# Hybrid decoder block: turned tiles leave PSUM first, a second turn stands elsewhere, one weight form is added on VectorE, and the last norm is regrouped

## The chip, the cores and the metric

The kernel runs on one core of one Trainium2 chip. The metric is the device time of one execution in microseconds (us), the median of several runs. TensorE (PE in the profile) multiplies, VectorE (DVE) and ScalarE (ACT) do the elementwise work, GpSimd (POOL) issues some DMAs here, and SyncE (SP) issues the rest. Each engine takes its own instructions strictly in order and waits on semaphores for the others.

## What is computed

One decoder block over 512 tokens of width 1024 in float32, and a final RMSNorm. The reference, cut to its frame and to the part in which the change lies:

```python
def swiglu(u, w_gate_up, w_down):          # FF = 2816
    gate, up = jnp.split(u @ w_gate_up, 2, axis=-1)
    return (jax.nn.silu(gate) * up) @ w_down

def reference(x, mem, ...):
    h = x
    for l in range(DEPTH):                 # DEPTH = 1
        h = h + hybrid_mixer(rmsnorm(h, mix_norm[l]), ...)
        h = h + memory_cross_attention(rmsnorm(h, xattn_norm[l]), rmsnorm(mem, mem_norm[l]), ...)
        h = h + swiglu(rmsnorm(h, ffn_norm[l]), w_gate_up[l], w_down[l])
    return rmsnorm(h, final_norm)
```

## The kernel before

The mixer and the attention fill the first 425 us or so, the feed-forward part and the last norm the rest. The mixer and the attention are not touched. Every product of two float32 matrices is taken in three matmuls: each operand is split in a high part and the rest, and high by high, high by rest and rest by high are summed in PSUM. For the weights `split_unit` does this with a ScalarE cast (`whi`, L194) and a VectorE subtraction (`wlo`, L196).

**The feed-forward part saves an eighth of its matmuls.** Each product of 2x2 blocks is computed by seven block products in place of eight. The seven need weight *forms* that are sums of quarters of the weight, and *forms* of the activations, which `forms` makes (L1116 on). Gate and up are computed in five blocks g0 to g4 of 512 columns each and a narrow block g5 of 256. The down product is taken in three parts, d0 after g1, d1 after g3, d2 after g5. The matmuls of both carry line L1046, and write PSUM tiles called gA, gB, gC and dA, dB, dC.

**Weight forms.** For one chunk of the weights, `load_strassen` loads the forms 1, 2 and 4 as they are (quarters 11, 12, 22), by DMAs that SP issues. Forms 5 and 7 are a load by SP and a second DMA that POOL issues and that adds to what lies there (L171). Form 6 is form 1 plus form 5, where form 1's tile is overwritten: a DMA from tile to tile that adds, issued by POOL as soon as form 2 is split (L202). Form 3 is form 2 plus form 6, a VectorE addition (L189). The whole narrow block lies in one chunk.

**Turns.** The products of silu(gate) and up lie with tokens on the partitions, and the down product wants them turned. `i_turnff` (Y in the list below) turns half a block: eight TensorE transposes (L1105, `ffT`) from the tiles `t_gu` into a PSUM tile of 128 by 1024 with the tag pd. Of this tag there is **one buffer**, so that the next turn waits until everything that reads the last has ended. ScalarE copies the second half out as `fb` (L1110); `forms` reads the first half (`FA`) straight from PSUM, in the cast L1122, in the subtractions L1131 and L1126, and last in L1141.

**Order.** The list `SPEC` says slot by slot which items are issued; each slot's matmuls stand in program order, and the elementwise work that follows an item (`post`), the loads and the splits of the next slot are written between them. Within that, a scheduler of the language places the instructions of each engine. `U:b.f` is product f of gate block b, `d:p.f` of down part p, `Y:b.i` the turn of half i of block b, `G` the load of the last gain.

**The last norm.** `i_down` adds each finished product to the residual `h` (L1202, L1204). When a half row of 128 tokens is finished, `half_done` squares it on ScalarE with a sum beside it and multiplies it by the gain (L1225). When both halves are, `final` turns the two sums to a factor (L1243, L1244, Ln, Exp, and one corrective step L1248 to L1250), scales both halves and stores them. The four token groups c = 0 to 3 are finished by product 7 (c = 2, 3) and product 4 (c = 0, 1).

Of the kernel before, what the change touches and what calls it, by code (L numbers as in the profile page):

```python
# [7 lines left out]
F32 = mybir.dt.float32  # L8
F32R = mybir.dt.float32r
AF = mybir.ActivationFunctionType  # L10
ALU = mybir.AluOpType
AX = mybir.AxisListType

P = 128
S = 512
DM = 1024
# [6 lines left out]
EPS = 1e-6  # L23
# [7 lines left out]
CHUNKS = [("g", b, ks, 512) for b in range(5) for ks in ((0, 1), (2, 3))] + [("g", 5, (0, 1, 2, 3), 256)]  # L31
# [25 lines left out]
]  # L57

# [2 lines left out]
def hybrid_block(ctx: ExitStack, tc: tile.TileContext, a: dict, out: bass.AP,  # L61
                 act_bufs=69, la=1, wb=(6, 4, 5), eng="", dact=(0, 1), raw_n=6, warm=12, spec=None, start=START, smm=START_MM, hu=1, dbg=None):
    nc = tc.nc
# [5 lines left out]
    small = ctx.enter_context(tc.tile_pool(name="small", bufs=4))  # L69
# [5 lines left out]
    def nm(base):  # L75
        uid[0] += 1
        return f"{base}_{uid[0]}"

    def T(base, dt=F32, n=512):
        return act.tile([P, n], dt, tag="a", name=nm("t_" + base))  # L80
# [101 lines left out]
    def split_unit(key):  # L182
        n = units[key][1]
        raw = ready[key]
        if key[0] == "s":
            c, f = key[1:]
            if f == 3:
                sw[c, 3] = sw.pop((c, 2))
                nc.vector.tensor_tensor(out=sw[c, 3][:, :n], in0=sw[c, 3][:, :n], in1=sw[c, 6][:, :n], op=ALU.add)  # L189
                yield  # L190
            raw = sw[c, f]
        hi = whi_p.tile([P, 1024], F32R, tag="hi", name=nm("whi"))
        lo = wlo_p.tile([P, 1024], F32R, tag="lo", name=nm("wlo"))
        nc.scalar.copy(hi[:, :n], raw[:, :n])  # L194
        yield
        nc.vector.tensor_tensor(out=lo[:, :n], in0=raw[:, :n], in1=hi.bitcast(F32)[:, :n], op=ALU.subtract)  # L196
        ready[key] = (hi, lo)
        if key[0] == "s" and f == 2:
            if (c, 5) not in sw:
                load_strassen(("s", c, 5))  # L200
            sw[c, 6] = sw.pop((c, 1))
            nc.gpsimd.dma_start(sw[c, 6][:, :n], sw[c, 5][:, :n], accum_op=ALU.add)  # L202
        yield
# [46 lines left out]
    sw = {}  # L250

    st = {}
# [842 lines left out]
    def i_turnff(b, i):  # L1095

        it = Item()

        def mm():
            it.ps = psum.tile([P, 1024], F32, tag="pd", name=nm("ffT"), bufs=1)  # L1100
            for k in (1, 0):
                for c in range(2):
                    for tt in range(2):
                        o = 512 * k + 256 * c + P * tt
                        nc.tensor.transpose(it.ps[:, o:o + P], st["fft", b, k, tt][:, (2 * i + c) * P:(2 * i + c + 1) * P],  # L1105
                                            ident)

        def post():
            fb = T("fb")
            nc.scalar.copy(fb, it.ps[:, 512:1024])  # L1110
            yield from forms("ff", 2 * b + i, it.ps[:, 0:512], fb)

        it.mm, it.post = mm, post
        return it

    def forms(x, i, FA, FB):  # L1116

        lo_, hi_ = slice(0, 256), slice(256, 512)

        def cast(base, src, w=None):  # L1120
            h = T(base, F32R)
            nc.scalar.copy(h if w is None else h[:, w], src)  # L1122
            return h

        def rest(dst, src, h):
            nc.vector.tensor_tensor(out=dst, in0=src, in1=h.bitcast(F32), op=ALU.subtract)  # L1126

        H1 = cast("xh", FA)
        H4 = cast("xq", FB[:, hi_], lo_)
        M = T("x57")  # L1130
        nc.vector.tensor_tensor(out=M[:, lo_], in0=FA[:, lo_], in1=FB[:, lo_], op=ALU.subtract)  # L1131
        nc.vector.tensor_tensor(out=M[:, hi_], in0=FB[:, hi_], in1=FB[:, lo_], op=ALU.subtract)  # L1132
        yield
        L1 = T("xl", F32R)
        rest(L1, FA, H1)
        st["X", x, 1, i], st["X", x, 2, i] = (H1[:, lo_], L1[:, lo_]), (H1[:, hi_], L1[:, hi_])
        H2 = cast("xh", M)
        N = T("x64")
        nc.vector.scalar_tensor_tensor(out=N[:, lo_], in0=M[:, lo_], scalar=-1.0, in1=FB[:, hi_],
                                       op0=ALU.mult, op1=ALU.subtract)  # L1140
        nc.vector.scalar_tensor_tensor(out=N[:, hi_], in0=N[:, lo_], scalar=-1.0, in1=FA[:, hi_],  # L1141
                                       op0=ALU.mult, op1=ALU.subtract)
        yield
        H3 = cast("xh", N)
        L2 = T("xl", F32R)
        rest(L2, M, H2)
        st["X", x, 5, i], st["X", x, 7, i] = (H2[:, lo_], L2[:, lo_]), (H2[:, hi_], L2[:, hi_])
        yield
        rest(H4[:, hi_], FB[:, hi_], H4[:, lo_])
        st["X", x, 3, i] = H4[:, lo_], H4[:, hi_]  # L1150
        L3 = T("xl", F32R)
        rest(L3, N, H3)
        st["X", x, 6, i], st["X", x, 4, i] = (H3[:, lo_], L3[:, lo_]), (H3[:, hi_], L3[:, hi_])
# [36 lines left out]
    def i_down(p, f, part=None):  # L1190
        it, ends, _ = product("d", p, f, part)

        def post():
            r, k, sign = INTO[f]
            last = p == 2
            if last and f == 2:
                st["pre"] = nc.scalar.preload_act_table_set("natural_log_exp_and_others")
                after(st["pre"], st["silu"])
            for tt in range(2):
                h = st["h", 2 * k + tt, r]  # L1200
                if sign > 0:
                    nc.vector.tensor_tensor(out=h, in0=h, in1=it.ps[tt], op=ALU.add)  # L1202
                else:
                    nc.vector.tensor_tensor(out=h, in0=h, in1=it.ps[tt], op=ALU.subtract)  # L1204
                if last and f in (2, 3):
                    half_done(2 * k + tt, r)
                elif last and f in (7, 4):
                    final(2 * k + tt)
            yield

        it.post = post if ends else None
        return it

    def number():

        st["n"] = st.get("n", -8) + 8
        if st["n"] == 0:
            st["numbers"] = T("numbers")
        return st["numbers"][:, st["n"]:st["n"] + 1]

    def half_done(c, r):
        h = st["h", c, r]
        q = number()
        nc.scalar.activation(T("sq"), h, AF.Square, accum_out=q)
        nc.vector.tensor_tensor(out=h, in0=h, in1=st["G"][r], op=ALU.mult)  # L1225
        st["ss", c, r] = q

    def i_gain():
        def prep():
# [5 lines left out]

        return Item(prep=prep)

    def final(c):
        half_done(c, 1)
        v = number()  # L1240
        y = number()
        w = number()
        nc.vector.tensor_scalar(out=v, in0=st["ss", c, 0], scalar1=1.0 / DM, scalar2=EPS, op0=ALU.mult, op1=ALU.add)  # L1243
        nc.vector.scalar_tensor_tensor(out=v, in0=st["ss", c, 1], scalar=1.0 / DM, in1=v, op0=ALU.mult, op1=ALU.add)  # L1244
        ln = nc.scalar.activation(y, v, AF.Ln)
        after(ln, st["pre"])
        nc.scalar.activation(y, y, AF.Exp, scale=-0.5)
        nc.vector.scalar_tensor_tensor(out=w, in0=v, scalar=y, in1=y, op0=ALU.mult, op1=ALU.mult)  # L1248
        nc.vector.tensor_scalar(out=w, in0=w, scalar1=-0.5, scalar2=1.5, op0=ALU.mult, op1=ALU.add)
        nc.vector.tensor_tensor(out=w, in0=w, in1=y, op=ALU.mult)  # L1250
        rows = slice(c * P, (c + 1) * P)
        for r in range(2):
            o = st["h", c, r]
            if r == 0:
                nc.scalar.activation(o, o, AF.Copy, scale=w)
            else:
                nc.vector.tensor_scalar(out=o, in0=o, scalar1=w, scalar2=None, op0=ALU.mult)
            nc.sync.dma_start(out[rows, 512 * r:512 * r + 512], o)

    def rm(r):  # L1260
        return Item(mm=r.mm, post=r.post)
# [17 lines left out]
    for line in (spec or SPEC):  # L1279
        its = []  # L1280
        for tok_ in line.split():
            name, _, arg = tok_.partition(":")
# [167 lines left out]
```

## Time and profile before

| | |
|---|---|
| median of 3 runs | 815.14 us (814.6 to 816.63) |
| the profiled execution | 817.78 us; its span, first to last instruction, 816.1 us |
| mean granted TensorE clock | 0.990 of full speed |
| busy share of the span | PE 97%, DVE 76%, ACT 59%, POOL 6% |
| chain that ended last | PE 75%, DVE 10%, DMA 7%, rest 8% |

The profile is a list of the engines' instructions in one execution, with start, length, and for idle time ahead of an instruction the length and the instruction that ended it. Starts are in us from the span's start. Matmuls overlap, so that the distance of two starts is the cost of one, and not the length shown.

### The profile page before, as it was taken

How to read it: one execution, taken by the hardware profiler on the slowest of the kernel's cores; microseconds unless marked ns; L12 is line 12 of the kernel's file. 1: busy time of each engine (PE TensorE's matmuls, PEld its weight loads, DVE VectorE, ACT ScalarE, POOL GpSimd, SP SyncE). 2: the span in 40 equal slices, each digit the busy share in tenths (PEclk: the TensorE clock that was granted, in tenths of full speed). 3: DMA queues.
4: the chain of work that ended last, by engine and by line, in shares of the span. 5: the costliest groups of instructions: out<-in, count | busy, mean ns of one | idle time of the engine just before them, and what ended most of it. 6: DMA issues, size and time to landing. Idle time of an engine off the chain costs nothing.

```text
span 816.1 us, 10514 instructions
## 1 busy us (share of the span) xinstructions
PE 791.6 (97%) x3856; PEld 666.0 (82%) x3856; DVE 617.5 (76%) x912; ACT 482.1 (59%) x768; POOL 45.6 (6%) x61
## 2 busy tenths in 40 slices
PE   9999999999999999999999999989999989999795
PEld 7888888888888889888888888878888767888684
DVE  7989979999875896355746667869657878665897
ACT  8667699567853555344635784744454835353664
POOL 0000000000000000000010001110101110101000
PEclk9999999999999999999999999999999999999899
DMA  8253415243573236223355367877887867977502
GB/s 324 86 168 104 146 55 174 65 150 100 194 250 120 81 107 192 89 78 104 129 113 145 78 207 183 235 175 190 197 256 161 256 163 178 225 221 170 138 14 103
DMA packets 40275, 124.95 MB, mean 153 GB/s; under 512 B 4752, under 2 KB 7184, under 8 KB 40224
## 3 DMA queue, kind: packets, MB, share of 16 engines
q1 hardware_dynamic: 32880, 98.33, 36.2%
q0 software_dynamic: 7344, 25.96, 17.5%
q8 instruction: 30, 0.49, 0.2%
q14 instruction: 21, 0.17, 0.1%
HBM read 113.48 MB, written 2.13 MB: 142 GB/s over the span
## 4 chain that ended last, share of the span: by engine, by line
PE 75%; DVE 10%; DMA 7%; issue 3%; ACT 3%; POOL 0%; SPq 0%; POOLq 0%; DVEq 0%; ACTq 0%
PE gA L1046 10%; PE dA L1046 5%; PE gB L1046 5%; DMA wq<-raw 4%; PE gC L1046 3%; DVE wlo L196 3%; PE v L117 2%; PE v L118 2%; PE v L116 2%; PE dB L1046 2%; DMA raw<-w_s 2%; PE op L116 2%; PE op L118 2%; PE wo L116 2%; PE wo L118 2%
## 5 line engine op out<-in xcount | busy, mean ns | idle before, releaser
L194 ACT CAST whi<-raw 128x1024 fp32r<-128x1024 f32 (+1 forms) x127 | 131.6, 1040 | 135.4 <-issue 25.6
L196 DVE TENSOR_TENSOR wlo<-raw,whi 128x1024 fp32r<-128x1024 f32 (+1 forms) x127 | 152.8, 1209 | 64.4 <-ACT whi L194 60.9
L194 ACT CAST whi<-wq 128x1024 fp32r<-128x1024 f32 (+1 forms) x68 | 69.2, 1025 | 64.2 <-PE gA L1046 20.4
L196 DVE TENSOR_TENSOR wlo<-wq,whi 128x1024 fp32r<-128x1024 f32 (+1 forms) x68 | 80.4, 1190 | 33.3 <-ACT whi L194 33.0
L1046 PE MATMUL gA<-whi,t_xh 128*128 128x512 f32 (+1 forms) x192 | 72.5, 378 | 0.0
L1046 PE MATMUL gA<-whi,t_xl 128*128 128x512 f32 (+1 forms) x192 | 72.1, 375 | 0.0
L1046 PE MATMUL gA<-wlo,t_xh 128*128 128x512 f32 (+1 forms) x192 | 72.0, 375 | 0.0
L171 POOL DMA_DIRECT2D raw<-w_s x34 | 29.3, 862 | 656.0 <-DVE t_Pl L232 406.2
L1046 PEld LDWEIGHTS gA<-whi,t_xh 128*128 128x128 f32 x192 | 36.9, 192 | 6.6 <-ACT t_gu L1068 0.4
L1046 PEld LDWEIGHTS gA<-wlo,t_xh 128*128 128x128 f32 x192 | 36.8, 192 | 6.3
L1046 PEld LDWEIGHTS gA<-whi,t_xl 128*128 128x128 f32 x192 | 36.9, 192 | 6.1
L189 DVE TENSOR_TENSOR wq<-wq,wq 128x1024 f32<-128x1024 f32 (+1 forms) x17 | 20.3, 1193 | 24.1 <-DMA wq<-raw 23.9
L1046 PE MATMUL dA<-whi,t_xl 128*128 128x512 f32 x88 | 34.5, 392 | 0.9 <-DVE t_xl L1126 0.8
L1046 PE MATMUL dA<-whi,t_xh 128*128 128x512 f32 x88 | 34.2, 392 | 0.6 <-DVE t_numbers L1243 0.6
L1046 PE MATMUL dA<-wlo,t_xh 128*128 128x512 f32 x88 | 34.3, 390 | 0.0
L1062 ACT ACTIVATE t_gu<-t_gu,s 128x512 f32<-128x512 f32 (+1 forms) x24 | 16.3, 689 | 28.8 <-DVE t_gu L1058 28.8
L1046 PE MATMUL gB<-whi,t_xq 128*128 128x512 f32 (+1 forms) x96 | 27.7, 373 | 0.0
L1122 ACT CAST t_xh<-t_x 128x512 fp32r<-128x512 f32 x30 | 18.6, 619 | 13.2 <-DVE t_x L1132 6.5
L116 PE MATMUL z<-t_uh,whi 128*128 128x512 f32 x64 | 25.2, 394 | 0.2 <-ACT t_uh L224 0.2
L116 PE MATMUL wo<-t_oh,whi 128*128 128x512 f32 x64 | 25.2, 394 | 0.0
L116 PE MATMUL v<-t_uh,whi 128*128 128x512 f32 x64 | 25.1, 392 | 0.0
L116 PE MATMUL q<-t_hgh,whi 128*128 128x512 f32 x64 | 25.1, 392 | 0.0
(384 smaller groups left out, 2241.0 us busy)
## 6 DMA issues: line engine op xcount, KB each, us to landing
raw<-w_u SPq DMA_DIRECT2D x76, 512.0 KB, 3.3
raw<-w_s SPq DMA_DIRECT2D x48, 512.0 KB, 4.4
wq<-w_s SPq DMA_DIRECT2D x32, 512.0 KB, 5.7
raw<-w_s POOLq DMA_DIRECT2D x32, 512.0 KB, 6.7
wq<-raw POOLq DMA_DIRECT2D x16, 512.0 KB, 7.2
t_x<-xT SPq DMA_DIRECT2D x16, 256.0 KB, 5.4
t_abc<-d_acs SPq DMA_DIRECT2D x16, 256.0 KB, 4.5
out<-t_hT SPq DMA_DIRECT2D x8, 256.0 KB, 2.2
```

What stands on the lines that cost most here:

```text
L116: nc.tensor.matmul(ps, whi, xhi, start=start, stop=False)
L117: nc.tensor.matmul(ps, whi, xlo, start=False, stop=False)
L118: nc.tensor.matmul(ps, wlo, xhi, start=False, stop=stop)
L171: nc.gpsimd.dma_start(sw[c, f][:, :n], quad("11" if f == 7 else "22"), accum_op=ALU.add)
L189: nc.vector.tensor_tensor(out=sw[c, 3][:, :n], in0=sw[c, 3][:, :n], in1=sw[c, 6][:, :n], op=ALU.add)
L194: nc.scalar.copy(hi[:, :n], raw[:, :n])
L196: nc.vector.tensor_tensor(out=lo[:, :n], in0=raw[:, :n], in1=hi.bitcast(F32)[:, :n], op=ALU.subtract)
L1046: nc.tensor.matmul(it.ps[tt], p[:, ts_], w[:, ws], start=first, stop=(c, i, n) == pairs[-1] and p is xh and w is wl, skip_group_check=True)
L1062: st["silu"] = nc.scalar.activation(g, g, AF.Silu, scale=st["r3",][:, c:c + 1])
L1122: nc.scalar.copy(h if w is None else h[:, w], src)
```

## The change

Four edits:

- `i_turnff` copies both halves of the turned tile out of PSUM on ScalarE, `fb` and then `fa`, and `forms` reads only these copies. It is one more copy of 128 by 512 in each of the eleven turns.
- In `SPEC`, the second turns Y:1.1 and Y:3.1 stand one slot earlier, so that TensorE runs them ahead of dB's first matmuls and no longer behind them. Y:4.1 stands one slot later, behind all of form 6's gA matmuls of the narrow block and no longer among them.
- In the narrow block, form 6 is added by VectorE (a new line 189) just ahead of its split; the DMA at L202 is left out there. It stays in all other blocks.
- The last norm keeps its numbers in a small tile of its own. The first half row's sum is scaled (a `tensor_scalar`) where it is made; token groups 2 and 3 are finished by one chain on two columns, after both; groups 0 and 1 by one chain each as before.

```diff
-    "d:0.1.0 Y:1.0", "d:0.2.0", "d:0.5.0 Y:1.1", "d:0.1.2 d:0.2.2", ...
+    "d:0.1.0 Y:1.0", "d:0.2.0 Y:1.1", "d:0.5.0", "d:0.1.2 d:0.2.2", ...
...
-    "U:5.1", "U:5.2 Y:4.0", "U:5.5 Y:4.1", "U:5.6", "U:5.3", "U:5.7", "U:5.4 G",
+    "U:5.1", "U:5.2 Y:4.0", "U:5.5", "U:5.6 Y:4.1", "U:5.3", "U:5.7", "U:5.4 G",
...
             c, f = key[1:]
+            if f == 6 and (c, 6) not in sw:
+                sw[c, 6] = sw.pop((c, 1))
+                nc.vector.tensor_tensor(out=sw[c, 6][:, :n], in0=sw[c, 6][:, :n], in1=sw[c, 5][:, :n], op=ALU.add)
+                yield
             if f == 3:
...
-        if key[0] == "s" and f == 2:
+        if key[0] == "s" and f == 2 and CHUNKS[c][:2] != ("g", 5):
...
         def post():
-            fb = T("fb")
-            nc.scalar.copy(fb, it.ps[:, 512:1024])
-            yield from forms("ff", 2 * b + i, it.ps[:, 0:512], fb)
+            F = T("fa"), T("fb")
+            for k in (1, 0):
+                nc.scalar.copy(F[k], it.ps[:, 512 * k:512 * k + 512])
+            yield
+            yield from forms("ff", 2 * b + i, *F)
...
-                if last and f in (2, 3):
+                if last and f in (2, 3, 7, 4):
                     half_done(2 * k + tt, r)
-                elif last and f in (7, 4):
-                    final(2 * k + tt)
+                if last and f == 4:
+                    final([2 * k + tt])
+            if last and f == 7:
+                final([2, 3])
...
+        if r == 0:
+            nc.vector.tensor_scalar(out=q, in0=q, scalar1=1.0 / DM, scalar2=EPS, op0=ALU.mult, op1=ALU.add)
...
-    def final(c):
-        half_done(c, 1)
...
+    def final(cs):
+        v, y, w, p = [st["s4"][:, o + cs[0]:o + cs[-1] + 1] for o in (4, 8, 12, 16)]
+        nc.vector.scalar_tensor_tensor(out=v, in0=v, scalar=1.0 / DM, in1=st["s4"][:, cs[0]:cs[-1] + 1],
+                                       op0=ALU.mult, op1=ALU.add)
```

The same move as in the first line is made for Y:3.1 in d1. From line 187 on, lines of the changed kernel have a number higher by 4 (up to 1108), and by 6 in `forms`.

VectorE's order in the narrow block, before. `whi` and `wlo` are the two parts of a weight form, `wq` the tile that form 6 is made in, `t_gu` gate and up:

```order
L1087 SCALAR_TENSOR_TENSOR t_gu_6476<-gA_6450,s_4271,t_gu_6476 128x512
L196 TENSOR_TENSOR wlo_6758<-raw_6608,whi_6757 128x1024
L1087 SCALAR_TENSOR_TENSOR t_gu_6478<-gA_6451,s_4271,t_gu_6478 128x512
L196 TENSOR_TENSOR wlo_6811<-wq_6566,whi_6810 128x1024
L189 TENSOR_TENSOR wq_6573<-wq_6573,wq_6566 128x1024
L1058 TENSOR_TENSOR t_gu_6751<-t_gu_6751,gC_6761 128x256
```

And now, at the same place:

```order
L1091 SCALAR_TENSOR_TENSOR t_gu_6492<-gA_6466,s_4271,t_gu_6492 128x512
L189 TENSOR_TENSOR wq_6582<-wq_6582,raw_6624 128x1024
L200 TENSOR_TENSOR wlo_6773<-raw_6624,whi_6772 128x1024
L1091 SCALAR_TENSOR_TENSOR t_gu_6494<-gA_6467,s_4271,t_gu_6494 128x512
L200 TENSOR_TENSOR wlo_6831<-wq_6582,whi_6830 128x1024
L193 TENSOR_TENSOR wq_6589<-wq_6589,wq_6582 128x1024
L1062 TENSOR_TENSOR t_gu_6766<-t_gu_6766,gC_6776 128x256
```

The addition of form 6 (the new L189) came in ahead of form 5's split; the rest keeps its order.

ScalarE's order a little later in the narrow block, around the first turn (`ffT`), before:

```order
L194 CAST whi_6888<-wq_6573 128x1024
L1062 ACTIVATE t_gu_6751<-t_gu_6751,s_4271 128x256
L194 CAST whi_6929<-raw_6651 128x1024
L1062 ACTIVATE t_gu_6753<-t_gu_6753,s_4271 128x256
L1110 COPY t_fb_6798<-ffT_6787 128x512
L1122 CAST t_xh_6800<-ffT_6787 128x512
L1122 CAST t_xq_6802<-t_fb_6798 128x256
```

And now:

```order
L198 CAST whi_6881<-wq_6589 128x1024
L1066 ACTIVATE t_gu_6766<-t_gu_6766,s_4271 128x256
L198 CAST whi_6928<-raw_6667 128x1024
L1066 ACTIVATE t_gu_6768<-t_gu_6768,s_4271 128x256
L1115 COPY t_fb_6814<-ffT_6802 128x512
L1115 COPY t_fa_6813<-ffT_6802 128x512
L1128 CAST t_xh_6823<-t_fa_6813 128x512
L1128 CAST t_xq_6825<-t_fb_6814 128x256
```

The second copy stands directly behind the first, and the cast behind it reads the copy.

TensorE's order around the second turn of the narrow block, before (the turn stands behind 9 of form 6's 24 gA matmuls) and then now (behind all 24):

```order
L1046 MATMUL gA_6725<-whi_6810,t_xh_4342 128x256
L1046 MATMUL gA_6725<-whi_6810,t_xl_4347 128x256
L1046 MATMUL gA_6725<-wlo_6811,t_xh_4342 128x256
L1105 MATMUL ffT_6856<-ident,t_gu_6562 128x128
L1105 MATMUL ffT_6856<-ident,t_gu_6564 128x128
```

```order
L1050 MATMUL gA_6741<-whi_6830,t_xh_4453 128x256
L1050 MATMUL gA_6741<-whi_6830,t_xl_4458 128x256
L1050 MATMUL gA_6741<-wlo_6831,t_xh_4453 128x256
L1109 MATMUL ffT_6909<-ident,t_gu_6578 128x128
L1109 MATMUL ffT_6909<-ident,t_gu_6580 128x128
```

Fifteen gA matmuls moved from behind the turn to ahead of it.

## Rows read from the trace of the kernel before

**Rows 1.** The page, part 1: busy time, share and instructions of each engine.

```profile
PE 791.6 (97%) x3856; PEld 666.0 (82%) x3856; DVE 617.5 (76%) x912; ACT 482.1 (59%) x768; POOL 45.6 (6%) x61
```

**Rows 2.** PE's waits: who waited for whom, us in total, times, longest.

```profile
PE ffT L1105 <- DVE t_x L1141: 6.2, 2, 5.6
PE ffT L1105 <- DVE t_gu L1087: 5.9, 2, 3.3
```

**Rows 3.** Timeline of PE, narrow block: start, length, engine, line, [idle <- releaser].

```profile
752.72 1.04 PE L1105 MATMUL ffT<-ident,t_gu 128*128 128x128 f32 x8
753.51 0.36 PE L1046 MATMUL gB<-whi,t_xh 128*128 128x256 f32 x1
...
757.42 0.28 PE L1046 MATMUL gA<-wlo,t_xh 128*128 128x256 f32 x1
763.26 1.94 PE L1105 MATMUL ffT<-ident,t_gu 128*128 128x128 f32 x8 [5.57 <-DVE t_x L1141]
...
768.20 0.52 PE L1046 MATMUL gB<-whi,t_xq 128*128 128x256 f32 x2
...
779.93 1.03 PE L1105 MATMUL ffT<-ident,t_gu 128*128 128x128 f32 x8
```

**Rows 4.** Timeline of DVE, narrow block.

```profile
746.71 1.23 DVE L196 TENSOR_TENSOR wlo<-raw,whi 128x1024 fp32r<-128x1024 f32 x1 [1.16 <-ACT whi L194]
...
754.48 1.23 DVE L196 TENSOR_TENSOR wlo<-wq,whi 128x1024 fp32r<-128x1024 f32 x1 [5.88 <-ACT whi L194]
...
762.70 0.41 DVE L1141 SCALAR_TENSOR_TENSOR t_x<-t_x,ffT 128x256 f32<-128x256 f32 x1
```

**Rows 5.** Timeline of ACT, narrow block.

```profile
753.40 1.05 ACT L194 CAST whi<-wq 128x1024 fp32r<-128x1024 f32 x1 [6.72 <-DMA wq<-raw]
...
760.01 0.57 ACT L1110 COPY t_fb<-ffT 128x512 f32<-128x512 f32 x1
```

**Rows 6.** Timeline of POOL, narrow block: the issue of form 6's DMA.

```profile
746.11 1.06 POOL L202 DMA_DIRECT2D wq<-raw  x1
```

**Rows 7.** Busy time by stretch: length, PE, PEld, DVE, ACT, POOL, clock, DMA share, GB/s.

```profile
746.71:754.48 7.77, 7.77 (x66) 7.70 (x65) 1.89 (x3) 1.08 (x2) 0.47 (x1) 1.00 0.74 138
754.48:779.93 25.45, 19.88 (x134) 18.85 (x134) 21.31 (x35) 16.34 (x28) 1.71 (x2) 0.87 0.44 114
```

**Rows 8.** DVE's groups by line and form: count, busy us, mean ns, idle before.

```profile
L189 DVE TENSOR_TENSOR wq<-wq,wq 128x1024 f32<-128x1024 f32 x16 | 19.6, 1225 | 24.1 <-DMA wq<-raw 23.9
...
L1131 DVE TENSOR_TENSOR t_x<-ffT,t_fb 128x256 f32<-128x256 f32 x11 | 4.6, 421 | 0.2
...
L1131 DVE TENSOR_TENSOR t_x<-t_fa,t_fb 128x256 f32<-128x256 f32 x4 | 1.7, 418 | 0.0
```

**Rows 9.** ACT's groups by line and form: the copy out of PSUM.

```profile
L1110 ACT COPY t_fb<-ffT 128x512 f32<-128x512 f32 x11 | 6.4, 585 | 8.3 <-PE ffT L1105 8.2
```

**Rows 10.** Timeline of PE in gate block g3, at its second turn.

```profile
639.04 0.39 PE L1046 MATMUL gB<-wlo,t_xh 128*128 128x512 f32 x1
640.05 1.06 PE L1105 MATMUL ffT<-ident,t_gu 128*128 128x128 f32 x8 [0.62 <-DVE t_x L1141]
```

**Rows 11.** Timeline of PE in d0 (first row) and d1 (the others).

```profile
549.95 0.42 PE L1046 MATMUL dB<-whi,t_xh 128*128 128x512 f32 x1
...
669.48 0.90 PE L1105 MATMUL ffT<-ident,t_gu 128*128 128x128 f32 x3 [3.31 <-DVE t_gu L1087]
...
682.19 0.50 PE L1046 MATMUL dA<-whi,t_xl 128*128 128x512 f32 x1 [0.79 <-DVE t_xl L1126]
```

**Rows 12.** Timeline of ACT in d0: the copy after the first turn.

```profile
545.84 0.59 ACT L1110 COPY t_fb<-ffT 128x512 f32<-128x512 f32 x1 [2.91 <-PE ffT L1105]
```

**Rows 13.** Timeline of DVE at the end.

```profile
802.52 0.68 DVE L1204 TENSOR_TENSOR t_hT<-t_hT,dA 128x512 f32<-128x512 f32 x1
...
808.26 0.68 DVE L1204 TENSOR_TENSOR t_hT<-t_hT,dA 128x512 f32<-128x512 f32 x1
...
811.79 0.48 DVE L1257 TENSOR_SCALAR t_hT<-t_hT,t_numbers 128x512 f32<-128x512 f32 x1
```

More of the change, by code (lines that the diff above doesn't have):

```diff
@@ L1212, in i_down @@
         return it
[L1214 to L1219, printed above, removed]
     def half_done(c, r):
         h = st["h", c, r]
-        q = number()
+        if (c, r) == (0, 0):
+            st["s4"] = small.tile([P, 32], F32, tag="s4", name="s4", bufs=1)
+        q = st["s4"][:, 4 * r + c:4 * r + c + 1]
         nc.scalar.activation(T("sq"), h, AF.Square, accum_out=q)
         nc.vector.tensor_tensor(out=h, in0=h, in1=st["G"][r], op=ALU.mult)
-        st["ss", c, r] = q
+        if r == 0:
+            nc.vector.tensor_scalar(out=q, in0=q, scalar1=1.0 / DM, scalar2=EPS, op0=ALU.mult, op1=ALU.add)
     def i_gain():
@@ L1236, in i_gain @@
         return Item(prep=prep)
-    def final(c):
-        half_done(c, 1)
[L1240 to L1244, printed above, removed]
+    def final(cs):
+        v, y, w, p = [st["s4"][:, o + cs[0]:o + cs[-1] + 1] for o in (4, 8, 12, 16)]
+        nc.vector.scalar_tensor_tensor(out=v, in0=v, scalar=1.0 / DM, in1=st["s4"][:, cs[0]:cs[-1] + 1],
+                                       op0=ALU.mult, op1=ALU.add)
         ln = nc.scalar.activation(y, v, AF.Ln)
@@ L1247, in final @@
         nc.scalar.activation(y, y, AF.Exp, scale=-0.5)
-        nc.vector.scalar_tensor_tensor(out=w, in0=v, scalar=y, in1=y, op0=ALU.mult, op1=ALU.mult)
-        nc.vector.tensor_scalar(out=w, in0=w, scalar1=-0.5, scalar2=1.5, op0=ALU.mult, op1=ALU.add)
[L1250 to L1258, printed above, removed]
+        if len(cs) == 1:
+            nc.vector.scalar_tensor_tensor(out=w, in0=v, scalar=y, in1=y, op0=ALU.mult, op1=ALU.mult)
+        else:
+            nc.vector.tensor_tensor(out=w, in0=v, in1=y, op=ALU.mult)
+            nc.vector.tensor_tensor(out=w, in0=w, in1=y, op=ALU.mult)
+        nc.vector.tensor_scalar(out=w, in0=w, scalar1=-0.5, scalar2=1.5, op0=ALU.mult, op1=ALU.add)
+        nc.vector.tensor_tensor(out=p, in0=w, in1=y, op=ALU.mult)
+        for c in cs:
+            rows = slice(c * P, (c + 1) * P)
+            r_ = st["s4"][:, 16 + c:17 + c]
+            for r in range(2):
+                o = st["h", c, r]
+                if r == 0:
+                    nc.scalar.activation(o, o, AF.Copy, scale=r_)
+                else:
+                    nc.vector.tensor_scalar(out=o, in0=o, scalar1=r_, scalar2=None, op0=ALU.mult)
+                nc.sync.dma_start(out[rows, 512 * r:512 * r + 512], o)
     def rm(r):
```

4 rows, old and new, of the table SPEC are left out of this document.

## The prediction

> **What bounds the kernel now.** I read the page's busy shares first. TensorE is busy 97% of the span [rows 1], so little is to be had except where it waits, and an edit counts only if it shortens one of its waits. The view of PE's waits, read next, names two kinds in the feed-forward part: turns (ffT) that wait for the last VectorE read of the turn before, L1141, 6.2 us in two places, and turns that wait for L1087, 5.9 us in two places [rows 2]. The timelines of the three engines then show the largest, in the narrow block. TensorE ends its ninth gA matmul, which starts at 757.42, and stands until the second turn at 763.26; after the wait its matmuls run at half pace until 768.20 [rows 3], and the granted clock of the stretch is 0.87 against 1.00 in the stretch before [rows 7].
>
> Backwards from there. L1141 starts at 762.70 because VectorE did nothing for 5.88 us before 754.48, waiting for a cast [rows 4]. ScalarE had waited 6.72 us with that cast for form 6's DMA [rows 5], which POOL issued at 746.11 [rows 6]; it was 7.3 us on its way. VectorE had 1.89 us of work in 7.77 us [rows 7]. So one DMA keeps two engines idle, the turn's copies stand behind it on both (ScalarE reaches its copy only at 760.01 [rows 5], though the first turn began at 752.72 [rows 3]), and with one pd buffer TensorE pays.
>
> **What that wait costs.** Without it: 33 matmuls go from 753.51 to 757.42 [rows 3], 0.12 us each. A turn takes 0.79 (752.72 to 753.51). From the ninth matmul to 768.20 there are that matmul, a turn and 15 matmuls: 0.12 + 0.79 + 0.08 of start-up + 15 x 0.12 = 2.8 us. It took 768.20 - 757.42 = 10.8. The wait with the slow matmuls behind it costs **8.0 us**.
>
> **Form 6 on VectorE.** The new addition costs 1.2 us, as L189 does now [rows 8]. It stands ahead of form 5's split, where VectorE now idles 1.16 us for a cast [rows 4]; so it costs next to nothing there, and if that cover were gone it would cost 1.2 us of a wait of 5.88 that is going anyway. The cast of form 6 can then follow about 747, its split about 748.5 in place of 754.48: **6.0 us earlier**. What L1141 had behind it moves with it.
>
> **Copies first, Y:4.1 later.** The pd buffer is now free after two copies; 0.59 us each [rows 9], some 0.48 from start to start (the read of the first overlaps the second). After the first turn ScalarE still has two activations of gC's products to do, so I put the copies at 754.2 to 755.3. TensorE comes to the second turn, which is now behind 15 more matmuls, at 757.54 + 1.8 = 759.34: four us to spare. The second turn waits for nothing, and 8.0 us go. Copies alone would not do it: behind the DMA they would end at 760.01 + 1.07 = 761.1.
>
> **What is late next there.** VectorE had 21.31 us of work in the 25.45 us from 754.48 to 779.93 [rows 7], at whose end TensorE starts the block's last turn [rows 3], which needs VectorE's last product. Starting 6.0 earlier, at 748.5, VectorE is done at 769.8 if it never waits, and at 773.95 if all its waits stay. TensorE would be there at 779.93 - 8.0 = 771.9, the middle of the two. I take 0.3 us for that tie: **-7.7**.
>
> Does it pay that the forms now read SBUF? L1131 takes 421 ns with the operand in PSUM and 418 ns with both in SBUF [rows 8]: nothing. [...]
>
> **g3.** Its second turn waits 0.62 us for the same L1141; from the matmul before it, it is 1.01 us, where two follow in 2 x 0.12 (a 128x512 has twice the columns) [rows 10]. The copies free the buffer some 3 us before. **-0.8**. The other gate block's turns have no wait shown; nothing.
>
> **d0 and d1.** Their first turns wait for L1087 (d1: 3.31 us and a slow stretch behind it [rows 11]). L1087 stands on VectorE behind L189, which waits for form 6's DMA; that is the 23.9 us at L189 [rows 8]. There the DMA stays, and VectorE's order up to it too: 0, with 1.2 us (one VectorE instruction more or less ahead of the DMA's issue) either way in each block. The second turns go ahead of dB. Their transposes wait for the first turn's copies: in d0 ScalarE starts them at 545.84 [rows 12], so they end about 546.9, and TensorE comes at 549.95 [rows 11]. Three us to spare, with nothing lost. The 0.79 wait of dA in d1 [rows 11] is for a subtraction that hangs on VectorE's L189 again and does not come earlier, but two more matmuls that need only the high part now stand ahead of it: 2 x 2 x 0.12, **-0.45**.
>
> **The other copies.** Eleven more copies, 11 x 0.585 = 6.4 us [rows 9], on an engine busy 59% [rows 1]. Each form becomes usable 0.48 us later than the turn. Between a turn and the first matmul on it stand at least twelve others; I cost it at nothing. Without that cover it would be 0.48 a turn.
>
> **The end.** VectorE's subtractions decide it: first at 802.52, last at 808.26, and from the last on the same chain as before to 811.79 and past it [rows 13]. Groups 2 and 3 now go through one chain, after both subtractions and both squares, in place of two that start one after the other; the last subtraction stands in order behind their scalings. Ahead of product 4 VectorE also has four small scalings of sums more, and a subtraction (0.6 to 0.7 us, the length of those shown) that stood behind a split now stands ahead of it, which moves product 4's first matmul. With the one subtraction's 0.68 us in full [rows 13] the end is 0.7 later; the chain on two columns adds some of the second subtraction that it waits for, at most another 0.68. I take the upper part between +0.5 and +1.4, **+1.1**, since VectorE has no idle time left at the end to hide either.
>
> **Sum:** -7.7 - 0.8 - 0.45 + 1.1 = -7.85. The profiled execution took 817.78, so 809.9; it lies 2.6 above the median of 815.14, and with that as base the forecast is **807.3 us**, 1.0% faster.
>
> **Rivals.**
> - *VectorE becomes the bound of the narrow block.* All its 4.1 us of small waits stay: it is done at 773.95, 2.0 us after TensorE, which with the slow matmuls after (8.0 lost for a gap of 5.7) is 2.8. For it: the slack is gone in the middle estimate. Against: some of those waits were for transfers and casts that now come earlier. 807.3 - 0.3 + 2.8 = 809.8. Chance 0.20.
> - *The waits of d0 and d1 shrink too.* Their VectorE order is rearranged around the last additions; were form 6's DMA issued one instruction of 1.2 us earlier in both, 2 x 1.2 x 1.4 = 3.4 us go: 803.9. Against: the instruction that releases the DMA keeps its place. Chance 0.12.
> - *A moved turn stalls TensorE.* In d0 or d1 it stands in TensorE's order ahead of twelve dB matmuls; if the first turn's copies end later than TensorE arrives, all of these wait. It decides from 3 us of delay in the copies, say by a cast that waits for dC and that ends up ahead of them. A stall costs between the 3.3 of the wait at d1's first turn [rows 11] and the narrow block's 8.0; I take the middle, 5.6. In one block: 812.9, within what counts as no change, chance 0.07. In both: 807.3 + 11.2 = 818.5, **slower**, chance 0.05. Against: the copies stand directly behind the turn in ScalarE's order.
>
> **How the numbers follow.** The forecast (805 to 809) has 0.56. About 0.3% (2.4 us) is the least that a measurement of this kernel can tell from no change: 812.7 to 817.6 is the same. Forecast, the VectorE rival and the shrinking waits are faster, 0.88; one stall is the same, 0.07; two are slower, 0.05. The range leaves out both stalls and half of the shrinking waits: 803.8 to 810.6.
>
> **What would show it.** In the changed kernel's PE timeline the narrow block has no wait at its second turn, and no slow matmuls follow; the waits for L1141 are gone from PE's list; those for L1087 remain, 5 to 7 us. VectorE has no 5.9 us gap in the narrow block. If the block's last turn waits for L1091 (L1087 before), the VectorE rival holds. If the last matmul and the span's end lie further apart by more than 1.4 us more than before, the end was mis-sized. It would be wrong above all if the second turn still waited, that is if ScalarE's copies came late.

## The result and the profile after

The changed kernel takes **809.26 us** (808.97 to 809.65, 4 runs) against 815.88 for the kernel before (814.6 to 818.1, 4 runs, the three of the table above and one more); the ratio is 0.9916, with a 95% interval of 0.9892 to 0.994. Beside later runs, against a kernel before of 817.32, the same program took 808.26, a ratio of 0.9894 (0.9878 to 0.991), where 0.990 to 0.993 was expected of this second measurement. So it is 0.8 to 1.1% faster; 1.0% was forecast (807.3 us, 803.8 to 810.6).

The profiled execution took 808.97, with a span of 807.3 us against 816.1. TensorE is as busy as it was, in less time. The page's busy shares, which answer [rows 1]:

```profile
PE 787.7 (98%) x3856; PEld 663.2 (82%) x3856; DVE 618.5 (77%) x910; ACT 487.2 (60%) x777; POOL 44.6 (6%) x60
```

PE's waits, which answer [rows 2]. Waits for the last read of a turn (L1141, now L1147) are gone from the list; those for L1087, now L1091, are still there, 6.5 us where they were 5.9:

```profile
PE ffT L1109 <- DVE t_gu L1091: 6.5, 2, 3.8
...
PE dA L1050 <- DVE t_hT L1210: 0.9, 1, 0.9
```

TensorE's timeline in the narrow block (start, length, engine, line), against [rows 3]:

```profile
751.07 1.04 PE L1109 MATMUL ffT<-ident,t_gu 128*128 128x128 f32 x8
...
757.57 0.28 PE L1050 MATMUL gA<-wlo,t_xh 128*128 128x256 f32 x1
757.69 1.03 PE L1109 MATMUL ffT<-ident,t_gu 128*128 128x128 f32 x8
...
770.37 1.03 PE L1109 MATMUL ffT<-ident,t_gu 128*128 128x128 f32 x8
```

The second turn follows the last gA matmul in 0.12 us, where it stood still for 5.57. From the first to the last turn the block takes 770.37 - 751.07 = 19.30 us; it took 779.93 - 752.72 = 27.21. VectorE and ScalarE in the same place, against [rows 4] and [rows 5]:

```profile
743.82 1.22 DVE L189 TENSOR_TENSOR wq<-wq,raw 128x1024 f32<-128x1024 f32 x1
745.07 1.23 DVE L200 TENSOR_TENSOR wlo<-raw,whi 128x1024 fp32r<-128x1024 f32 x1
...
746.87 1.22 DVE L200 TENSOR_TENSOR wlo<-wq,whi 128x1024 fp32r<-128x1024 f32 x1
...
769.40 0.48 DVE L1091 SCALAR_TENSOR_TENSOR t_gu<-gA,s,t_gu 128x256 f32<-128x256 f32 x1
```

```profile
745.34 1.05 ACT L198 CAST whi<-wq 128x1024 fp32r<-128x1024 f32 x1 [0.30 <-PE gA L1050]
...
752.56 0.56 ACT L1115 COPY t_fb<-ffT 128x512 f32<-128x512 f32 x1
753.03 0.58 ACT L1115 COPY t_fa<-ffT 128x512 f32<-128x512 f32 x1
```

The new addition, the split of form 5 and the split of form 6 stand close behind each other, with one L1091 between the last two; the cast of form 6 waits 0.30 us for a gA matmul, where it waited 6.72 for the DMA. Busy time over the block (length, PE, PEld, DVE, ACT, POOL, clock, DMA share, GB/s), after and then before:

```profile
751.07:770.37 19.30, 19.16 (x151) 18.29 (x150) 17.37 (x32) 15.49 (x27) 1.70 (x2) 1.00 0.49 125
```

```profile
752.72:779.93 27.21, 21.64 (x150) 20.61 (x149) 21.32 (x35) 17.42 (x29) 1.71 (x2) 0.87 0.41 107
```

TensorE's matmuls there took 21.6 us and now take 19.2: the granted clock, 0.87 on the mean of the block before, is 1.00 now. The slow matmuls (0.21 us from start to start, against 0.12 ahead of the wait) stood behind the wait and are gone with it.

Where the time went, cut at the starts of the turns in TensorE's timeline. A row is the difference of two such starts; the last ends with the span. The kernels of the experiments stand beside the two:

| us | d0's first turn to g3's first | g3's first to second | d1's first turn to g5's first | g5's first to d2's | d2's turn to the end |
|---|---|---|---|---|---|
| before | 90.98 | 7.15 | 87.25 | 27.21 | 36.17 |
| before, again | 91.24 | 7.03 | 87.13 | 27.09 | 36.13 |
| changed | 90.69 | 6.33 | 86.49 | 19.30 | 36.93 |
| changed, again | 90.60 | 6.36 | 85.99 | 19.30 | 36.89 |
| without form 6 on VectorE | 90.33 | 6.33 | 88.06 | 26.29 | 36.90 |
| without the second copy | 91.45 | 7.08 | 85.60 | 18.89 | 36.68 |
| turns in their old places | 90.77 | 6.33 | 86.05 | 20.35 | 36.98 |
| old last norm | 90.56 | 6.37 | 86.31 | 19.31 | 36.27 |
| before, with form 6 alone | 92.21 | 6.93 | 86.87 | 19.44 | 36.18 |
| changed, form 6 on VectorE in d0, d1 too | 86.44 | 6.34 | 81.32 | 19.32 | 36.90 |
| the same with the old last norm | 86.42 | 6.34 | 81.27 | 19.33 | 36.32 |
| before, form 6 on VectorE in g5, d0, d1 | 86.33 | 8.01 | 81.24 | 19.44 | 36.06 |
| changed, form 6 on VectorE in g5, d0, d1, d2 | 86.43 | 6.33 | 81.29 | 19.31 | 37.09 |

Between the first two lines of the changed kernel and the two of the kernel before, which are each one program run twice, the second column and the last two differ by 0.12 us at most, the first and third by up to 0.5. This is how far a single profile can be trusted in each column.

### The profile page after: what moved, and what is told of

Read it like the earlier page. It is cut to its first block, busy times and chain, and to the rows that moved or that the text cites. A ratio compares the mean times of both kernels' runs of the same rounds, so it can differ in the third digit from the quotient of the medians.

```text
span 807.3 us, 10509 instructions
## 1 busy us (share of the span) xinstructions
PE 787.7 (98%) x3856; PEld 663.2 (82%) x3856; DVE 618.5 (77%) x910; ACT 487.2 (60%) x777; POOL 44.6 (6%) x60
## 4 chain that ended last, share of the span: by engine, by line
PE 79%; DVE 8%; DMA 5%; ACT 3%; issue 3%; POOL 0%; SPq 0%; DVEq 0%; POOLq 0%; ACTq 0%
PE gA L1050 10%; PE dA L1050 5%; PE gB L1050 5%; DMA wq<-raw 3%; PE gC L1050 3%; PE dB L1050 3%; DVE wlo L200 3%; PE v L117 2%; PE v L118 2%; PE v L116 2%; PE dC L1050 2%; PE wo L118 2%; PE op L118 2%; PE wo L116 2%; PE op L116 2%
## 5 line engine op out<-in xcount | busy, mean ns | idle before, releaser
L200 DVE TENSOR_TENSOR wlo<-raw,whi 128x1024 fp32r<-128x1024 f32 (+1 forms) x127 | 152.5, 1210 | 58.7 <-ACT whi L198 58.2
L200 DVE TENSOR_TENSOR wlo<-wq,whi 128x1024 fp32r<-128x1024 f32 (+1 forms) x68 | 80.3, 1190 | 24.5 <-ACT whi L198 24.4
L118 PE MATMUL z<-t_uh,wlo 128*128 128x512 f32 x64 | 25.0, 391 | 0.0
```

Of the source, the lines that this page charges most:

```text
L118: nc.tensor.matmul(ps, wlo, xhi, start=False, stop=stop)
```

## The experiments

The theory was that form 6's DMA, and not the one PSUM buffer by itself, held the narrow block. The rival was that copying out of PSUM is what counts.

**The kernel before, a second time.**

> The kernel before, unchanged, profiled a second time. It is run because its times spread over 3.5 us (814.6 to 818.1) and those of the changed kernel over 0.7 (808.97 to 809.65). Theory: the spread is the narrow block's; form 6's DMA, on whose arrival everything there hangs, is quicker or slower from execution to execution. Then the wait at the second turn (5.57 us in the first profile) comes out different here, by about as much as the time differs, and the waits of d0 and d1 (2.63 and 3.31) about the same. Rival: the spread is in d0 and d1, whose turns wait for the same kind of DMA and which both kernels have; then those two waits differ and the narrow block's stays within 0.3 us.

It took 817.28 us, 0.5 less than the first profile's 817.78. PE's timeline, d0, d1 and the narrow block:

```profile
545.17 0.55 PE L1105 MATMUL ffT<-ident,t_gu 128*128 128x128 f32 x3 [2.90 <-DVE t_gu L1087]
...
669.20 0.90 PE L1105 MATMUL ffT<-ident,t_gu 128*128 128x128 f32 x3 [3.23 <-DVE t_gu L1087]
...
762.89 1.51 PE L1105 MATMUL ffT<-ident,t_gu 128*128 128x128 f32 x6 [5.53 <-ACT whi L194]
```

The narrow block's wait is the same to 0.04 us; d0's differs by 0.27, d1's by 0.08. That speaks against the theory on the spread, but the two executions are only 0.5 us apart, so what makes the spread of 3.5 us stays open. The narrow block's wait is no accident of one execution. The profile names a cast of ScalarE as its releaser here, and VectorE's L1141 in the first profile; in that profile the two end within 0.01 us of each other (at 763.12 and 763.11), and of the two only L1141 reads the turned tile.

**Without form 6 on VectorE.** The condition on the chunk is taken out, so that the DMA is issued in the narrow block too and the addition on VectorE falls away:

```diff
-        if key[0] == "s" and f == 2 and CHUNKS[c][:2] != ("g", 5):
+        if key[0] == "s" and f == 2:
```

> The changed kernel with form 6 of the narrow block again added by a DMA; copies, places of the turns and last norm as changed. Theory (the DMA holds the narrow block): ScalarE's copies end at about 761 in the clock of the first profile while TensorE comes to the second turn at 759.3, and VectorE starts its 21 us of work 6 us later, so that the block's last turn waits for L1091: 4 to 7 us slower than the changed kernel, 813 to 816 us. Rival (the one PSUM buffer holds it, and copying out is what counts): at most 2 us slower, 809.3 to 811.3 us, with a wait below 2 us at the second turn and none at the last.

It took 816.56 us (814.58 to 817.44), a ratio to the kernel before of 0.9987 (0.9976 to 0.9997): nearly the whole gain is gone. The narrow block takes 26.29 us, 7.0 more than in the changed kernel; d1 takes 1.6 to 2.1 more, with a first wait of 4.63 us. POOL, ScalarE and TensorE there:

```profile
743.82 1.06 POOL L206 DMA_DIRECT2D wq<-raw  x1
```

```profile
752.92 1.05 ACT L198 CAST whi<-wq 128x1024 fp32r<-128x1024 f32 x1 [6.86 <-DMA wq<-raw]
...
760.01 0.59 ACT L1115 COPY t_fa<-ffT 128x512 f32<-128x512 f32 x1
...
763.55 1.04 ACT L198 CAST whi<-wq 128x1024 fp32r<-128x1024 f32 x1
```

```profile
760.65 1.10 PE L1109 MATMUL ffT<-ident,t_gu 128*128 128x128 f32 x8 [1.76 <-ACT t_fa L1115]
764.64 0.80 PE L1050 MATMUL dA<-whi,t_xh 128*128 128x512 f32 x1 [2.90 <-ACT whi L198]
```

The DMA's tile is cast 9.1 us after the issue (743.82 to 752.92). The wait at the second turn is shorter than before, 1.76 us in place of 5.57; of the 3.8 us, 1.8 are the fifteen matmuls (0.12 us each) that now stand ahead of the turn, and the rest goes with the copies. But ScalarE is still late from the DMA on, and TensorE stands 2.90 us for the next cast instead. The theory said that the rest of the wait would come back at L1091, ahead of the block's last turn; it came back at a cast, 4 us after the second turn, and the last turn (778.40) waits for nothing. The loss, 7.3 and 8.3 us against the two medians of the changed kernel, was expected as 4 to 7.

**Without the second copy.** `forms` reads the first half from PSUM, as before:

```diff
-            F = T("fa"), T("fb")
-            for k in (1, 0):
-                nc.scalar.copy(F[k], it.ps[:, 512 * k:512 * k + 512])
-            yield
-            yield from forms("ff", 2 * b + i, *F)
+            fb = T("fb")
+            nc.scalar.copy(fb, it.ps[:, 512:1024])
+            yield from forms("ff", 2 * b + i, it.ps[:, 0:512], fb)
```

> The changed kernel, but forms reads the first half of the turned tile straight from PSUM again, as before; form 6 on VectorE, the places of the turns and the last norm as changed. Theory (the DMA holds the narrow block): with form 6 early, L1147 ends about 757 and the second turn, due at 759.3, finds the buffer free; only g3's 0.8 us comes back, and in d0 and d1 the moved turns just fit (buffer free at 549.7, TensorE there at 550): 0.8 to 1.5 us slower than the changed kernel, 810 to 811 us. Rival (copying out is what counts): most of the narrow block's 7.9 us comes back, 814 us or more.

It took 808.65 us (808.02 to 808.98), ratio 0.9889 (0.9872 to 0.9905), against 0.9894 for the changed kernel beside the later runs: no difference that can be told, where 0.8 to 1.5 us was expected. VectorE's last read of the first turn, and TensorE's second turn, in the narrow block:

```profile
755.72 0.41 DVE L1145 SCALAR_TENSOR_TENSOR t_x<-t_x,ffT 128x256 f32<-128x256 f32 x1
```

```profile
757.93 0.28 PE L1050 MATMUL gA<-wlo,t_xh 128*128 128x256 f32 x1
758.05 1.04 PE L1109 MATMUL ffT<-ident,t_gu 128*128 128x128 f32 x8
```

With form 6 early the buffer is free at 756.13, two us before it is wanted. In g3 the wait came back as expected (7.08 against 6.33); the narrow block gained 0.4, and what d0 lost d1 won: their first waits are 3.50 and 2.79 us here.

**Turns in their old places.**

```diff
-    "d:0.2.0 Y:1.1", "d:0.5.0",      "d:1.2.0 Y:3.1", "d:1.5.0",      "U:5.5", "U:5.6 Y:4.1",
+    "d:0.2.0", "d:0.5.0 Y:1.1",      "d:1.2.0", "d:1.5.0 Y:3.1",      "U:5.5 Y:4.1", "U:5.6",
```

> The changed kernel with the three turns back in their old slots; copies, form 6 on VectorE and last norm as changed. Theory: in the narrow block the copies end at about 755.3 and the second turn's old place comes at 757.5, so no wait returns there; in d1 the two matmuls that stood ahead of the wait are gone again, 0.5 to 1.1 us slower than the changed kernel over d0 and d1, 809.8 to 810.4 us. Rival (the fifteen gA matmuls ahead of the second turn are what covers it): a wait of over 1.5 us at the narrow block's second turn, 811 us or more.

It took 809.59 us (806.92 to 810.31), ratio 0.9896 (0.9876 to 0.9916), no different from the changed kernel that can be told. In d0 and d1, where 0.5 to 1.1 us were expected, the lengths (90.77 and 86.05) lie within 0.2 us of one or both executions of the changed kernel; what the moves are worth beside the varying waits is worked out below. In the narrow block 1.05 us are lost, not at the second turn but later:

```profile
764.67 0.39 PE L1050 MATMUL gA<-whi,t_xh 128*128 128x256 f32 x1 [1.23 <-ACT t_gu L1072]
```

**Form 6 alone**, put into the kernel before.

> The kernel before with one edit alone: form 6 of the narrow block added on VectorE. Theory: nearly all of the change is in this edit. With form 6 early L1145 (L1141 before) ends about 757, the second turn at its old place is due at 757.5, and the narrow block from its first to its last turn takes 19 to 20.5 us in place of 27.2: ratio 0.990 to 0.9925. Rival (it needs the copies or the later turn too): the second turn waits for L1145 and slow matmuls follow, 22 us or more from first to last turn, ratio 0.994 or above.

It took 809.87 us (809.05 to 810.86), ratio 0.9912 (0.989 to 0.9934), and the narrow block 19.44 us: one edit gives what the whole change gives there. VectorE's last read of the first turn, and TensorE:

```profile
757.57 0.42 DVE L1145 SCALAR_TENSOR_TENSOR t_x<-t_x,ffT 128x256 f32<-128x256 f32 x1
```

```profile
757.98 0.28 PE L1050 MATMUL gA<-wlo,t_xh 128*128 128x256 f32 x1
758.13 1.06 PE L1109 MATMUL ffT<-ident,t_gu 128*128 128x128 f32 x8
```

The read ends at 757.99, the turn starts at 758.13, at its old place: it just fits.

With form 6 early, the four profiles give the narrow block 19.30 us with copies and the later turn, 18.89 with the later turn alone, 20.35 with the copies alone and 19.44 with neither. So there the later turn is worth 0.55 to 1.05 us, and the copies cost 0.4 to 0.9.

**The old last norm.**

> The changed kernel with the last norm as before, all else as changed. From the narrow block's last turn to the span's end it took 36.17 us before and 36.93 in the changed kernel. Theory (the regrouped chain costs that, most of it at the start of product 4): 36.0 to 36.5 us here, 0.4 to 0.9 us faster than the changed kernel. Rival (the 0.76 us come from the copies, which make the last turn's forms 0.48 us later on a VectorE without idle time, and the regrouping costs nothing or gains): 36.8 us or more here.

From the last turn to the end it takes 36.27 us, against 36.93 and 36.89; the regrouping costs 0.65 us in the profile, and the copies the remaining 0.1. The median, 809.1 us (806.64 to 809.76; ratio 0.9899, 0.9877 to 0.9921), is not below the changed kernel's 808.26; the run below with d0's and d1's waits gone settles that.

**Form 6 on VectorE in d0 and d1 too.** The changed kernel's waits for L1091 have VectorE waiting ahead of them for the same kind of DMA, so the same edit was tried there:

```diff
-        if key[0] == "s" and f == 2 and CHUNKS[c][:2] != ("g", 5):
+        if key[0] == "s" and f == 2 and c not in (10, 11, 12, 13, 14):
```

> The changed kernel with form 6 on VectorE in the down parts d0 and d1 too (four chunks), where a DMA adds it and VectorE waits for that DMA ahead of L1091. Theory (the same DMA is what makes the first turns of d0 and d1 wait): both waits (2.75 and 3.77 us) and the slow matmuls behind them go, 5 to 10 us, at 4 x 1.2 us of VectorE work in idle time: 799 to 805 us. Rival (VectorE is full there, so its additions take the place of the wait): less than 2.5 us faster than the changed kernel, with L1091 still what the first turns wait for.

It took **799.35 us** (799.19 to 799.59), ratio 0.9785 (0.977 to 0.9801): 8.9 us below the changed kernel. d0 in VectorE's timeline, in the changed kernel and then here:

```profile
537.26 0.75 DVE L1091 SCALAR_TENSOR_TENSOR t_gu<-gA,s,t_gu 128x512 f32<-128x512 f32 x1
542.52 1.22 DVE L193 TENSOR_TENSOR wq<-wq,wq 128x1024 f32<-128x1024 f32 x1 [4.52 <-DMA wq<-raw]
543.67 1.22 DVE L200 TENSOR_TENSOR wlo<-raw,whi 128x1024 fp32r<-128x1024 f32 x1
544.80 0.75 DVE L1091 SCALAR_TENSOR_TENSOR t_gu<-gA,s,t_gu 128x512 f32<-128x512 f32 x1
```

```profile
536.90 0.74 DVE L1091 SCALAR_TENSOR_TENSOR t_gu<-gA,s,t_gu 128x512 f32<-128x512 f32 x1
537.56 1.22 DVE L189 TENSOR_TENSOR wq<-wq,raw 128x1024 f32<-128x1024 f32 x1
538.76 1.23 DVE L200 TENSOR_TENSOR wlo<-raw,whi 128x1024 fp32r<-128x1024 f32 x1
539.90 0.75 DVE L1091 SCALAR_TENSOR_TENSOR t_gu<-gA,s,t_gu 128x512 f32<-128x512 f32 x1
```

The addition of 1.22 us stands where VectorE waited 4.52, the second L1091 comes 4.9 us sooner (4.5 counted from the first), and TensorE's turn (541.78 here) waits for nothing. Of PE's waits in the feed-forward part one is left, at the end:

```profile
PE dA L1050 <- DVE t_hT L1210: 1.0, 1, 1.0
```

**The same with the old last norm.**

> The changed kernel with form 6 on VectorE in d0 and d1 too, and with the last norm as before. The profiles so far give 36.3 us from the last turn to the span's end with the old last norm (36.27) and 36.9 with the regrouped one (36.93, 36.89), but the medians of the two kernels did not show that (809.1 against 808.26). Theory (the regrouping costs 0.6 us and the medians differed by the waits at the DMAs of d0 and d1, which are gone here): 36.1 to 36.4 us at the end and 798.4 to 799.1 us in all, against 799.35. Rival (what the end gains is lost ahead of it): 799.3 us or more.

It took **798.5 us** (798.24 to 799.04), ratio 0.977 (0.9752 to 0.9789), with 36.32 us at the end. Against the regrouped norm (799.35, and 799.45 in the last run below, which stood beside this one) it is 0.9 faster; the theory holds, and this is the fastest kernel of the study.

**The kernel before with form 6 on VectorE in g5, d0 and d1**, no copies, no moved turns, the old norm:

> The kernel before with one edit: form 6 on VectorE in the narrow block, d0 and d1. Forms read PSUM, the turns stand in their old places, the last norm is the old one. Theory (the DMA of form 6 is what all the large waits hung on; the copies are worth g3's 0.7 us, the moved turns at most 0.5 in each of d0 and d1, the regrouping minus 0.6): 799 to 801 us, ratio 0.978 to 0.981, with no wait for L1091 or L1145 over 1 us. Rival (with less waiting on DMAs the one PSUM buffer becomes the bound, and the copies and moved turns earn their keep): the second turns of d0, d1 or the narrow block wait over 1 us each, 802 us or more.

It took 800.12 us (799.71 to 800.25), ratio 0.9787 (0.9769 to 0.9805). The theory wanted no wait for L1145 over 1 us; one is there, not at the turns that the rival named but in g3:

```profile
634.35 0.39 PE L1050 MATMUL gB<-wlo,t_xh 128*128 128x512 f32 x1
636.25 1.06 PE L1109 MATMUL ffT<-ident,t_gu 128*128 128x128 f32 x8 [1.51 <-DVE t_x L1145]
```

That is 8.01 against 6.34 us in g3, and it is the whole distance of 1.6 us to the kernel just above: without the copies g3 loses twice what it lost in the kernel before (7.15). d0, d1 and the narrow block are the same within 0.12 us with and without copies and moved turns.

**Form 6 on VectorE in d2 as well.**

> The changed kernel with form 6 on VectorE in d0, d1 and d2. In d2 VectorE works without a gap up to the last subtraction, and the DMAs there land long before they are wanted. Theory (an addition moved to VectorE pays only where VectorE waits for the DMA): against 799.35 with d0 and d1 alone, 1.0 to 2.0 us slower (1.2 for the chunk of 1024 columns and 0.7 for that of 512), 800.3 to 801.4, with the end 38 to 39 us after the last turn. Rival (the additions fit in the few waits on casts at d2's start): within 0.5 us of 799.35.

It took 799.45 us (799.14 to 799.75), ratio 0.978 (0.9762 to 0.9798). The theory is wrong here: 1.9 us of VectorE work more, in a part where VectorE seemed full, made the end 0.2 us later (37.09 against 36.90), and nothing in the median. VectorE takes most of it in ahead of the end: the split (L200) behind both additions starts 10.05 us after d2's turn (770.86 against 760.81), where it starts 9.85 us after it with d0 and d1 alone (770.45 against 760.60). The changed kernel's VectorE has gaps for it, 1.06 us in the narrow block and 0.32 and 0.25 us before d2's first subtractions.

## Why the prediction was right

**The wait and its cause.** Right. 8.0 us were to go from the narrow block, and 7.91 went (27.21 to 19.30). Taking form 6's DMA back in brings 7.0 of them back; taking it out alone gives 7.8. The steps can be laid beside each other, the block starting 1.65 us earlier by then (751.07 against 752.72): form 6's split was put at 748.5, which is 746.85 here, and stands at 746.87; the copies at 754.2 to 755.3, so 752.55 to 753.65, and are at 752.56 to 753.61; the second turn at 759.34, so 757.69, where it is. That they meet to 0.02 us is in part luck, since two of them were put down as about.

**Copies alone.** Their end was put at 761.1 with the DMA left in; in the run without form 6 on VectorE, whose block starts 0.61 us earlier, the copy ended at 760.60. But what follows from them was read too well: with form 6 early they are not needed in the narrow block, as the runs without the second copy and with form 6 alone show. The prediction gave the wait to both edits together; it is form 6's.

**VectorE's tie.** VectorE's last product ends at 769.88, TensorE's turn comes at 770.37: no wait, half a us to spare. Of the 0.3 us taken for it 0.1 was lost, and by the times not to VectorE: TensorE's first matmul behind the second turn starts at 758.87, 1.18 us after the turn where a turn takes 0.79, just behind a cast of ScalarE that ends at 758.82. The run without the second copy has no such gap and is 0.4 faster there. The rival that VectorE becomes the bound did not come about.

**Reading SBUF in place of PSUM.** Right: nothing was counted for it. L1131 took 421 ns with PSUM and takes 421 as L1137 from SBUF, L1141 took 415 and takes 420 as L1147, L1126 took 683 and takes 686 as L1132.

**g3.** Right: 0.8 was to go, 7.15 came to 6.33, and the wait comes back without the copies. TensorE's timeline, against [rows 10]:

```profile
638.94 0.40 PE L1050 MATMUL gB<-wlo,t_xh 128*128 128x512 f32 x1
639.17 1.04 PE L1109 MATMUL ffT<-ident,t_gu 128*128 128x128 f32 x8
```

**d0 and d1.** The first turns' waits stay, as said; after, against [rows 11]:

```profile
545.60 0.90 PE L1109 MATMUL ffT<-ident,t_gu 128*128 128x128 f32 x3 [2.75 <-DVE t_gu L1091]
...
669.06 0.90 PE L1109 MATMUL ffT<-ident,t_gu 128*128 128x128 f32 x3 [3.77 <-DVE t_gu L1091]
```

This is the term that was mis-sized: 0 was taken for d0 and -0.45 for the moved turn in d1, and the profile shows -0.29 and -0.76. That is not a shorter wait for the DMA, since d1's is longer than before (3.77 against 3.31). These waits vary, 2.4 to 3.5 us in d0 and 2.8 to 4.6 in d1 from run to run, also in the changed kernel's second execution, where nothing in the program differs:

```profile
545.35 0.55 PE L1109 MATMUL ffT<-ident,t_gu 128*128 128x128 f32 x3 [2.66 <-DVE t_gu L1091]
...
668.31 0.55 PE L1109 MATMUL ffT<-ident,t_gu 128*128 128x128 f32 x3 [3.29 <-DVE t_gu L1091]
```

So they have to be taken off first. Without its first wait, d0 is 88.35 and 88.34 us in the two executions of the kernel before, 87.94 in both of the changed kernel, and 88.14 with the turns in their old places; d1 is 83.94 and 83.90, then 82.72 and 82.70, then 82.96. By these profiles the moves are worth 0.2 us in d0 and 0.25 in d1. The rest of the difference to the kernel before, 0.2 and 0.9, comes without them, and what makes it stays open. With the DMA waits gone, old and new places agree within 0.1 us.

The granted clock behind the wait is not the same from execution to execution either. The first 10 us from d0's first turn in the kernel before, in the changed kernel and in its second execution (columns as above, the clock third from the end):

```profile
541.92:551.92 10.00, 7.37 (x30) 5.83 (x29) 8.22 (x12) 4.58 (x7) 1.71 (x2) 0.83 0.54 116
```

```profile
542.15:552.15 10.00, 7.25 (x34) 5.96 (x33) 8.13 (x12) 5.46 (x9) 1.71 (x2) 0.83 0.55 116
```

```profile
541.98:551.98 10.00, 7.34 (x41) 6.08 (x40) 8.19 (x12) 6.18 (x10) 1.71 (x2) 1.00 0.52 118
```

The waits are 2.63, 2.75 and 2.66 us, and the clock fell behind the first two (0.83) and not behind the third (1.00). The length of d0 without its first wait is 87.94 us either way in the changed kernel: where the clock stayed up, TensorE stood later on for another 1.25 us in d0, and 1.19 in d1, for the subtraction (L1132, L1126 before) for which dA waited 0.79 in d1 before [rows 11]. That wait, from which the -0.45 was taken, is absent in the changed kernel's first execution and there in its second.

Neither moved turn stalled TensorE, so the slower rival did not come about, nor did the one in which these waits shrink on their own.

**The end.** +1.1 was taken, between 0.5 and 1.4; it is +0.76 (36.17 to 36.93), of which the old norm takes 0.65 back. Two subtractions ahead of the chain on two columns were counted too high. VectorE's first and last subtraction and the last scaling, against [rows 13]:

```profile
793.40 1.28 DVE L1210 TENSOR_TENSOR t_hT<-t_hT,dA 128x512 f32<-128x512 f32 x2
...
799.45 0.68 DVE L1210 TENSOR_TENSOR t_hT<-t_hT,dA 128x512 f32<-128x512 f32 x1
...
802.98 0.48 DVE L1264 TENSOR_SCALAR t_hT<-t_hT,s 128x512 f32<-128x512 f32 x1
```

From the first to the last subtraction it is 6.05 us where it was 5.74, and the first comes 23.03 us after the last turn where it came 22.59: 0.3 of the chain, 0.4 of the work ahead of it.

**The sum.** By the profile -0.29 - 0.82 - 0.76 - 7.91 + 0.76 = -9.0, with +0.2 ahead of d0 -8.8; forecast -7.85; by the medians -6.6 and -9.1. The forecast lies between the two. As a time it rests on the first three runs of the kernel before; on the median of all four, 815.88, it would have been 808.0. The medians of the kernel before move by 1.5 us from set to set, more than the terms other than the narrow block's are worth.

## What to carry to other kernels

When a wait has two possible reasons, a late producer and a single buffer, follow the late one back first: with the producer early, the single buffer was free in time in the narrow block, and the other three edits were worth about 1 us or less each in this kernel. The buffer can still matter elsewhere: in g3 the copies are worth 0.8 us, and 1.7 once the waits of d0 and d1 are gone. Here a DMA that only adds one tile to another took 7.2 us on the median of 16 (up to 9.2) from issue to landing, and engines that stand in order behind its result waited for it (VectorE 23.9 us in all [rows 8], ScalarE 6.72 in the narrow block [rows 5]); where the engine that waits could do the addition in 1.2 us, let it, and look for the same pattern wherever that instruction's wait shows in the trace. And do not count moved and regrouped work as a gain until a run without it is slower: the regrouping cost 0.6 us, and the medians do not show the moved turns.

## What the runs showed that was not expected

- The same edit in four more chunks brought 9 us more, as much as the change itself, for 4 x 1.22 us of VectorE work in places where VectorE had waited. The two waits on which it rests (5.9 us of PE's waits, [rows 2]) stood beside the one that the change removes.
- A busy engine is not a full one: VectorE works from 787.17 to the first of the last subtractions without a gap in the kernel before, and yet 1.9 us more of additions cost 0.2: there are gaps ahead of that stretch to do them in (1.06, 0.32 and 0.25 us in the changed kernel).
- Taking one wait away can give most of it to the next in line: without form 6 on VectorE the second turn's wait fell by 3.8 us, by the copies and the later turn together, and the block by 0.8 to 0.9 (27.21 and 27.09 to 26.29).
- Of two executions of one program, with first waits in d0 within 0.1 us, one ran on at a lower granted clock (0.83 over the 10 us from d0's first turn) and the other did not (1.00), and without that first wait the block took the same time: the one at the higher clock stood 1.25 us at a later wait that the other did not have.
